# Where the low halves of the x forms are made, and which pairs take seven products: five edits to a decoder trunk in fp32

## The chip, the cores and the metric

One core of a Trainium2 chip. Its engines run each its own list of instructions and wait for each other through semaphores: PE (TensorE, matrix products), DVE (VectorE), ACT (ScalarE), POOL (GpSimd) and SP, which here only issues transfers. POOL and ACT issue transfers too. The metric is the device time of one execution in us; the lower the better.

## The reference

Two layers on 256 tokens of width 2048, all in fp32. Each is a token mixer (layer 0 HGRN2, layer 1 gated linear attention, GLA) beside a 4-head attention into 256 memory tokens, an output projection, and a SwiGLU feed-forward block (FFN) of width 5632:

```python
def reference(x, mem, ...):
    h = x
    for layer in range(2):
        hn = _rmsnorm(h, norm_mix[layer])
        y, xq = _hgrn2_mixer(hn, ...) if layer == 0 else _gla_mixer(hn, ...)
        xa = _memory_attention(xq, mem_n, w_mem_kv[layer])
        h = h + jnp.concatenate([y, xa], axis=-1) @ w_out[layer]

        hn = _rmsnorm(h, norm_ffn[layer])
        gate, up = jnp.split(hn @ w_gate_up[layer], 2, axis=-1)
        h = h + (jax.nn.silu(gate) * up) @ w_down[layer]
    return _rmsnorm(h, norm_final)
```

w_out is 2048 x 2048, w_gate_up 2048 x 11264, w_down 5632 x 2048; GLA's q and k are 768 columns each of its input projection.

## The kernel before

**Split operands.** PE multiplies a rounded form of fp32. So each operand is held as a high half (a rounded copy, made on ACT) and a low half (what the copy lost: a subtraction on DVE), and each product is three matmuls: xh by hi, xh by lo, xl by hi. A matmul takes 128 rows of K, one of the two tiles of 128 tokens and 512 columns of a weight (384 in GLA's q and k). This holds for weights (tiles "parts", line 300 and what calls it) and for activations.

**Pairs of K tiles and seven products.** 2048 rows of K are 16 tiles, taken as eight pairs 0 to 7. A pair's two K tiles, the two token tiles and two groups of columns (c0 and c1) are a product of 2 x 2 by 2 x 2 blocks. As eight products it costs 24 matmuls. As seven (Winograd's form of Strassen's scheme) it costs 21, for which sums and differences of the blocks are needed on both sides: of x once, of the weights for each pair and column group. A plan is a string that names the kind of each pair:

- "-": eight products; the four weight blocks are split in two operations each on ACT and on DVE (parts ..a, ..b).
- "S": seven products. `seven` splits one block (..a, 512 elements), two blocks (..b, 1024), then makes sums of blocks within the raw tile (512 and 1024 elements), and splits these (..c and ..d, 1024 each). Of pair 0's weights one sum comes from a load that accumulates into a tile T (POOL's queue).
- "H" and "O", in the FFN only: eight products that go into the same seven accumulators as S's, with a sum of weight blocks (H: ..a, ..b, a difference of 512, ..c of 512) or none (O).

The sums of a plan's S pairs share their accumulators, and after the last pair DVE adds these up into the four results (`early` in the output projection, `sums` in the FFN).

**The x forms of the FFN.** For each of the eight pairs `Forms` holds the four blocks of x and their sums and differences (eight forms for S, six for O, nine for B) with a high and a low half each, as PAIRS = "SSSSSOSB" says. `put` (line 394) gets the transposed blocks from PSUM, scales them on ACT into a staging tile g (tag "stg", two buffers), adds on DVE, makes the high half with one cast on ACT (hf_ph) and the low half with one subtraction on DVE (hf_pl). In names hf_3l is pair 3's low half. `h_forms` makes two pairs from 512 columns of h, as they come out of the output projection.

**The output projection.** In each layer: columns 0 to 511 by plain products (`one(0, ...)`, accumulators wo_0), then columns 512 to 1535 as pairs by the plan OUT (wo0p and wo1p), then columns 1536 to 2047 (`one(3, ...)`, wo_3), whose two sums are added into h by DVE as h<-wo_3. The forms of pairs 0 and 1 are made during the paired part, those of 2 to 5 during wo_3, and those of 6 and 7 need h's last columns, so they come during the first pairs of FFN block 0. For an S pair of OUT, the sums of the mixer's output y are made by `more_of`.

**The FFN.** `ffn` runs 11 blocks of 512 columns of gate and of up (`up_block`, accumulators f_p), each with the eight pairs in order by KINDS (one string for each of blocks 0 to 3, the last for 4 to 10). Weight pairs are numbered through the program: in layer 0 block 0 is parts84 (pair 0) to parts91 (pair 7), block 1 begins with parts92; in layer 1 block 0 is parts288 to 295. Between the blocks come parts of the down projection (fd). At the end of layer 0's FFN the last columns of the down projection go into h, and `h_quad` squares, transposes (tp_hm) and splits them for GLA's first projection (gx).

**What sets the order.** From pair 3 of block 0 on (`Engine.kept`, up to the end of the FFN's blocks), instructions keep the order of the code. Elsewhere a scheduler orders each engine's list at build time by its own estimate of times; in an engine's list an instruction that waits holds all that follow it. Small pieces of work are put in a queue (`later`), and `step`, called once or more for a pair, takes one off, or nothing where None was queued. Raw weight tiles have three buffers, the split "parts" six. Loads are issued by SP, except those that accumulate, which are POOL's.

## Time and profile before

| | |
|---|---|
| time before, median of 3 runs | 2253.98 us (2252.5 to 2254.8) |
| the profiled execution: own time, span | 2254.6 us, 2252.8 us |
| PE busy, matmuls | 2238.6 us (99%), 10668 |
| DVE busy, instructions | 2031.5 us (90%), 2551 |
| ACT busy, instructions | 1452.8 us (64%), 2010 |
| POOL busy, instructions | 280.4 us (12%), 275 |
| moved by DMA | 477.28 MB, mean 212 GB/s |
| mean granted clock of PE | 0.999 |

The span is that from the first to the last instruction. The busy time of an engine is the sum over its instructions, without those that issue transfers. Nearly every operation is recorded under line 151, a helper, so rows are told apart by the names of their tiles. A stage's state is read from the busy time in a stretch of the span, and from the waits in brackets: [0.49 <-ACT parts85b] means that an instruction's engine was idle 0.49 us before it and that ACT's result parts85b ended that.

### The profile page before, as it was taken

How to read it: one execution, taken by the hardware profiler on the slowest of the kernel's cores; microseconds unless marked ns; L12 is line 12 of the kernel's file. 1: busy time of each engine (PE TensorE's matmuls, PEld its weight loads, DVE VectorE, ACT ScalarE, POOL GpSimd, SP SyncE). 2: the span in 40 equal slices, each digit the busy share in tenths (PEclk: the TensorE clock that was granted, in tenths of full speed). 3: DMA queues.
4: the chain of work that ended last, by engine and by line, in shares of the span. 5: the costliest groups of instructions: out<-in, count | busy, mean ns of one | idle time of the engine just before them, and what ended most of it. 6: DMA issues, size and time to landing. Idle time of an engine off the chain costs nothing.

```text
span 2252.8 us, 30400 instructions
## 1 busy us (share of the span) xinstructions
PE 2238.6 (99%) x10668; PEld 1894.6 (84%) x10668; DVE 2031.5 (90%) x2551; ACT 1452.8 (64%) x2010; POOL 280.4 (12%) x275
## 2 busy tenths in 40 slices
PE   9999999999999999999999999999999999999998
PEld 7888888888888888888889999988888888888887
DVE  6879899898998999999996887889999999999997
ACT  7656656565666666666665665566566676666664
POOL 1000100000111112112210000000011221212110
PEclk9999999999999999999999999999999999999999
DMA  8656655656687778878865445566677878887874
GB/s 296 215 168 213 199 182 177 200 193 190 198 236 232 229 234 231 230 230 238 244 221 168 141 156 182 164 209 197 208 221 224 233 230 238 242 238 236 231 233 167
DMA packets 255628, 477.28 MB, mean 212 GB/s; under 512 B 18255, under 2 KB 47731, under 8 KB 255219
## 3 DMA queue, kind: packets, MB, share of 16 engines
q1 hardware_dynamic: 228547, 420.21, 55.5%
q0 software_dynamic: 25632, 50.87, 13.0%
q10 hardware_dynamic: 1296, 4.26, 0.5%
q8 instruction: 84, 1.38, 0.2%
q14 instruction: 69, 0.57, 0.1%
HBM read 472.12 MB, written 3.15 MB: 211 GB/s over the span
## 4 chain that ended last, share of the span: by engine, by line
PE 90%; DVE 6%; issue 2%; DMA 1%; ACT 1%; SPq 0%; POOL 0%; DVEq 0%; POOLq 0%; ACTq 0%
PE f_p L151 34%; PE fd L151 18%; PE wo L151 4%; PE m1p L151 2%; PE hv2p L151 2%; PE hv1p L151 2%; PE hf0p L151 2%; PE hv0p L151 2%; PE wo1p L151 2%; PE hf2p L151 2%; PE hf1p L151 2%; PE wo0p L151 2%; PE m0p L151 2%; PE gk0p L151 1%; PE gk1p L151 1%
## 5 line engine op out<-in xcount | busy, mean ns | idle before, releaser
L151 DVE TENSOR_TENSOR raw<-raw 128x1024 f32<-128x1024 f32 (+3 forms) x330 | 311.2, 943 | 16.7 <-DMA raw<-in_w_down_dram 5.6
L151 ACT CAST parts<-raw 128x1024 fp32r<-128x1024 f32 (+1 forms) x216 | 211.7, 1016 | 56.8 <-DMA raw<-in_w_down_dram 14.7
L151 DVE TENSOR_TENSOR parts<-raw,parts 128x1024 fp32r<-128x1024 f32 (+1 forms) x176 | 200.2, 1171 | 22.7 <-ACT parts L151 22.0
L444 POOL DMA_DIRECT2D raw<-in_w_gate_up_dram x92 | 80.4, 873 | 541.2 <-DMA raw<-in_w_gate_up_dram 274.7
L300 POOL TENSOR_TENSOR parts<-raw,parts 128x1024 fp32r<-128x1024 f32 x40 | 95.6, 2406 | 113.5 <-ACT parts L151 81.2
L151 ACT COPY h<-fd 128x512 f32<-128x512 f32 x80 | 45.7, 588 | 46.5 <-PE fd L151 44.0
L428 POOL DMA_DIRECT2D T<-in_w_gate_up_dram x36 | 21.1, 587 | 430.2 <-DVE hf_4g L151 82.7
L151 ACT ACTIVATE s<-s,rf_r 128x512 f32<-128x512 f32 x44 | 31.8, 723 | 42.0 <-DVE s L151 42.0
L151 DVE SCALAR_TENSOR_TENSOR s<-e,rf_r,s 128x512 f32<-128x512 f32 x44 | 45.7, 1076 | 2.9 <-ACT s L151 0.5
L151 DVE TENSOR_TENSOR e<-f_p,e 128x512 f32<-128x512 f32 x66 | 45.2, 684 | 2.6 <-DVE s L151 0.5
L429 POOL DMA_DIRECT2D T<-in_w_gate_up_dram x36 | 31.0, 861 | 120.4 <-DMA T<-in_w_gate_up_dram 111.1
L151 ACT COPY fd<-h 128x512 f32<-128x512 f32 x82 | 45.2, 582 | 0.0
L444 POOL DMA_DIRECT2D raw<-in_hgrn_w_in_dram x17 | 14.7, 867 | 209.9 <-DMA raw<-in_hgrn_w_in_dram 124.6
L151 PE MATMUL fd<-parts,s_0h 128*128 128x512 f32 x128 | 39.8, 392 | 0.0
L151 PE MATMUL fd<-parts,s_4h 128*128 128x512 f32 x128 | 39.8, 392 | 0.0
L151 PE MATMUL fd<-parts,s_8h 128*128 128x512 f32 x128 | 39.8, 392 | 0.0
L151 PE MATMUL fd<-parts,s_2h 128*128 128x512 f32 x128 | 39.8, 392 | 0.0
L151 PE MATMUL fd<-parts,s_6h 128*128 128x512 f32 x128 | 39.8, 392 | 0.0
L151 PE MATMUL fd<-parts,s_1h 128*128 128x512 f32 x128 | 39.4, 389 | 0.0
L151 PE MATMUL fd<-parts,s_3h 128*128 128x512 f32 x128 | 39.4, 389 | 0.0
L151 PE MATMUL fd<-parts,s_5h 128*128 128x512 f32 x128 | 39.4, 389 | 0.0
L151 PE MATMUL fd<-parts,s_7h 128*128 128x512 f32 x128 | 39.4, 389 | 0.0
(6020 smaller groups left out, 7434.0 us busy)
## 6 DMA issues: line engine op xcount, KB each, us to landing
raw<-in_w_gate_up_dram SPq DMA_DIRECT2D x224, 512.0 KB, 4.4
raw<-in_w_down_dram SPq DMA_DIRECT2D x80, 1024.0 KB, 5.5
raw<-in_w_gate_up_dram SPq DMA_DIRECT2D x220, 256.0 KB, 4.2
raw<-in_hgrn_w_in_dram SPq DMA_DIRECT2D x79, 512.0 KB, 4.6
raw<-in_gla_w_in_dram SPq DMA_DIRECT2D x96, 384.0 KB, 3.3
raw<-in_w_gate_up_dram POOLq DMA_DIRECT2D x92, 256.0 KB, 4.9
T<-in_w_gate_up_dram POOLq DMA_DIRECT2D x72, 256.0 KB, 5.0
raw<-in_w_out_dram SPq DMA_DIRECT2D x16, 1024.0 KB, 5.1
```

Source lines behind the costliest of these rows:

```text
L151: ins = func(*args, **kwargs)
L300: low = (nc.gpsimd if free_port else ve).tensor_tensor(out=both[:, 1, k:j, 0:m], in0=src[:, k:j, :], in1=both[:, 0, k:j, 0:m].bitcast(F32) ...
L428: nc.gpsimd.dma_start(out=both[:, 0, :], in_=rows[0])
L429: nc.gpsimd.dma_start(out=both[:, 0, :], in_=rows[1], accum_op=ALU.add)
L444: nc.gpsimd.dma_start(out=raw[:, 1, 0:n], in_=rows[1], accum_op=ALU.add)
```

## The change

Five edits:

1. In `Forms.put`, for kinds S and O (pairs 0 to 6), ACT writes -g into the low half beside the high half's sum, rounded as the high half is, and a DMA on POOL's queue, from SBUF to SBUF, then adds g to it. DVE's subtraction stays for pair 7 (kind B) alone. A transfer is 512 KB, for pair 5 (O) 384 KB. Since g has to live until its transfer has read it, the staging tiles of pairs 4, 5 and 6 are now tiles of other stages that are idle then ("v", "gate", "tq").
2. At the end of layer 0's FFN a None is queued ahead of the transposes of the third group of 512 columns, so these come a step later on PE.
3. GLA's q and k projections: one more pair is S, in both of them.
4. FFN block 0: pairs 2 and 4 go from H to S, in both layers.
5. The output projection: pair 7 of the plan goes from "-" to S, in both layers; the fourth S pair's forms of y are made by the `more_of` that is there, in the tile "Q".

```diff
--- before.py
+++ after.py
@@ -374,7 +374,7 @@
 
 
         def __init__(self, p, name):
-            self.kind = PAIRS[p]
+            self.p, self.kind = p, PAIRS[p]
             self.names = FACTORS[self.kind]
             n = len(self.names)
             th, tl = HOMES[p]
@@ -393,7 +393,9 @@
 
         def put(self, ps, gains):
 
-            g = work.tile([P, 8, P], F32, tag="stg", name=f"{self.name}g", bufs=2)
+            home = ("stg",) * 4 + ("v", "gate", "tq", "stg")
+            g = (opp if home[self.p] == "tq" else work).tile([P, 8, P], F32, tag=home[self.p], name=f"{self.name}g",
+                                                             **({"bufs": 2} if home[self.p] == "stg" else {}))
             for k in range(2):
                 ac.activation(out=g[:, 2 * k:2 * k + 2, :], in_=ps[:, 2 * k * P:(2 * k + 2) * P].rearrange(
                     "p (a t) -> p a t", t=P), func=AF.Copy, scale=gains[k])
@@ -401,7 +403,11 @@
 
             def parts(i, j, n):
                 ac.copy(out=self.h[:, i:i + n, :], in_=g[:, j:j + n, :])
-                tt(out=self.l[:, i:i + n, :], in0=g[:, j:j + n, :], in1=self.h[:, i:i + n, :].bitcast(F32), op=ALU.subtract)
+                if self.kind == "B":
+                    tt(out=self.l[:, i:i + n, :], in0=g[:, j:j + n, :], in1=self.h[:, i:i + n, :].bitcast(F32), op=ALU.subtract)
+                    return
+                ac.activation(out=self.l[:, i:i + n, :], in_=g[:, j:j + n, :], func=AF.Copy, scale=-1.0)
+                nc.gpsimd.dma_start(out=self.l[:, i:i + n, :].bitcast(F32), in_=g[:, j:j + n, :], accum_op=ALU.add)
 
             if self.kind == "O":
                 tt(out=g[:, 4:6, :], in0=g[:, 1:3, :], in1=g[:, 0:4:3, :], op=ALU.subtract)
@@ -672,7 +678,7 @@
     MANY = 12
 
 
-    def h_quad(hq, q, gain, ss, name, queue=later, sevens=SEVEN):
+    def h_quad(hq, q, gain, ss, name, queue=later, sevens=SEVEN, wait=False):
 
         for t in range(NT):
             square_sum(h[:, t, q * 512:(q + 1) * 512], ss[:, t, q:q + 1], f"{name}{q}{t}")
@@ -686,7 +692,7 @@
             hq[q] = Pairs(*both)
             hq.setdefault("pairs", {}).update({2 * q: both[0], 2 * q + 1: both[1]})
 
-        queue(turn)
+        queue(*([None] if wait else []), turn)
 
     def h_forms(forms, n, gain, ss, name):
 
@@ -1111,7 +1117,7 @@
                 nc.gpsimd.memset(dst[-1][:, :, :, DK:T], 0.0)
             return [lambda t, d=d: d[:, t, :, 0:DK] for d in dst]
 
-        project_two(hq["pairs"], ("------S-", "------S-")[pr], w, kw + pr * 2 * DK, pr * 2 * DK, 2 * DK, f"gk{pr}", give,
+        project_two(hq["pairs"], "-----SS-", w, kw + pr * 2 * DK, pr * 2 * DK, 2 * DK, f"gk{pr}", give,
                     lambda ps: ps.rearrange("p (a c) -> p a c", c=DK), fed=False)
         for d in dst:
             for t in range(NT):
@@ -1194,7 +1200,7 @@
     PARTS = ((0,), (1, 2), (3, 4), (5, 6), (7, 8), (9, 10))
 
 
-    KINDS = ("SHHSHOSO", "HHHSSOSO", "SHHSSOSO", "SSHSSOHS", "SSSSSOSS")
+    KINDS = ("SHSSSOSO", "HHHSSOSO", "SHHSSOSO", "SSHSSOHS", "SSSSSOSS")
 
 
 
@@ -1309,7 +1315,7 @@
 
     ENDS = (('0-1S2S3-',), ('0-1S2S3-',))
 
-    OUT = "4-5-2-0S6S7-3S1-"
+    OUT = "4-5-2-0S6S7S3S1-"
 
 
     flush()
@@ -1350,7 +1356,7 @@
         ss = new_ss(f"ss_n{l}")
         if l == 0:
             hq = {}
-            ffn(0, hq2, r2, lambda n: h_quad(hq, n, g_mix[1], ss, "hm1_", sevens=2))
+            ffn(0, hq2, r2, lambda n: h_quad(hq, n, g_mix[1], ss, "hm1_", sevens=2, wait=n == 2))
             scale = lambda ss=ss: h_scale(ss, "rm1", True)
         else:
             gf = []
```

(In OUT a digit is the pair, the sign behind it the kind: "7-" becomes "7S". The tile names y_7g and y_7m come from that part of y.)

The instructions move with it. First DVE in layer 0, at the end of the output projection and the beginning of block 0. Before:

```order
L151 SCALAR_TENSOR_TENSOR parts84c<-raw_4383,parts84c 128x512
L151 TENSOR_TENSOR parts84d<-raw_4383,parts84d 128x1024
L151 TENSOR_TENSOR hf_4l<-hf_4g,hf_4h 128x1024
L151 TENSOR_TENSOR hf_5l<-hf_5g,hf_5h 128x768
L151 TENSOR_TENSOR parts85a<-raw_4444,parts85a 128x1024
L151 TENSOR_TENSOR parts85b<-raw_4444,parts85b 128x1024
L151 TENSOR_TENSOR h<-wo_3_0_0_4179,h 128x512
L151 TENSOR_TENSOR h<-wo_3_0_1_4180,h 128x512
L151 TENSOR_TENSOR raw_4444<-raw_4444 128x512
L151 TENSOR_TENSOR parts86a<-raw_4499,parts86a 128x1024
L151 TENSOR_TENSOR parts85c<-raw_4444,parts85c 128x512
```

Now:

```order
L151 TENSOR_TENSOR raw_4405<-raw_4405 128x1024
L151 TENSOR_TENSOR h<-wo_3_0_0_4197,h 128x512
L151 TENSOR_TENSOR h<-wo_3_0_1_4198,h 128x512
L151 SCALAR_TENSOR_TENSOR parts84c<-raw_4405,parts84c 128x512
L151 TENSOR_TENSOR parts84d<-raw_4405,parts84d 128x1024
L151 TENSOR_TENSOR parts85a<-raw_4467,parts85a 128x1024
L151 TENSOR_REDUCE rf_red<-ss_f_3589 128x2
L151 TENSOR_TENSOR parts85b<-raw_4467,parts85b 128x1024
L151 TENSOR_SCALAR rf_v<-rf_red 128x2
L151 TENSOR_TENSOR parts86b<-raw_4522,parts86b 128x1024
```

parts84c's second half, parts84d, 85a and 85b stood ahead of the two adds h<-wo_3 and now stand behind them; the low halves hf_4l and hf_5l are gone. Three rows further on DVE's list now reads, with pair 86 as S:

```order
L151 SCALAR_TENSOR_TENSOR hf_6g<-hf_6g 128x128
L151 TENSOR_TENSOR hf_6g<-hf_6g 128x128
L151 TENSOR_TENSOR parts85c<-raw_4467,parts85c 128x512
L151 TENSOR_TENSOR parts86a<-raw_4522,parts86a 128x512
L151 TENSOR_TENSOR raw_4522<-raw_4522 128x512
L151 TENSOR_TENSOR raw_4522<-raw_4522 128x1024
L151 TENSOR_TENSOR hf_7g<-hf_7g 128x256
L151 SCALAR_TENSOR_TENSOR parts86c<-raw_4522,parts86c 128x1024
L151 SCALAR_TENSOR_TENSOR hf_7g<-hf_7g 128x128
L151 TENSOR_TENSOR parts86d<-raw_4522,parts86d 128x1024
L151 TENSOR_TENSOR hf_7g<-hf_7g 128x128
L151 TENSOR_TENSOR parts87a<-raw_4562,parts87a 128x512
```

No low half of hf_6 stands there any more; pair 86 takes six operations where as H it took four, and 88 likewise; parts88c comes 13 rows behind the last one shown.

Then ACT at the forms of pair 6 (hf_6hl holds both its halves). Before:

```order
L151 CAST parts85c<-raw_4444 128x512
L151 ACTIVATE junk_hf_31_4371,ss_f_3589<-h 128x512
L151 CAST parts86b<-raw_4499 128x1024
L151 ACTIVATE hf_6g<-tp_hf_6_4431,pv 128x256 x2
L151 CAST parts86c<-raw_4499 128x512
L151 CAST hf_6hl<-hf_6g 128x1024
L151 CAST parts87a<-raw_4536 128x512
L151 ACTIVATE hf_7g<-tp_hf_7_4483,pv 128x256 x2
L151 CAST parts87b<-raw_4536 128x1024
```

Now:

```order
L151 CAST parts85b<-raw_4467 128x1024
L151 CAST parts86b<-raw_4522 128x1024
L151 ACTIVATE hf_6g<-tp_hf_6_4453,pv 128x256 x2
L151 CAST parts85c<-raw_4467 128x512
L151 CAST hf_6hl<-hf_6g 128x1024
L151 ACTIVATE hf_6hl<-hf_6g 128x1024
L151 CAST parts86a<-raw_4522 128x512
L151 ACTIVATE hf_7g<-tp_hf_7_4506,pv 128x256 x2
L151 ACTIVATE parts86c<-raw_4522 128x1024
```

ACT makes both halves of hf_6, and the cast of 86a stands behind them; before, 86a's stood at the head, ahead of 85c's and 86b's.

## The prediction

> **What bounds the kernel now.** The totals come first, then the chain of waits, then the busy time by stage.
>
> ```profile
> PE 2238.6 (99%) x10668; PEld 1894.6 (84%) x10668; DVE 2031.5 (90%) x2551; ACT 1452.8 (64%) x2010; POOL 280.4 (12%) x275
> PE 90%; DVE 6%; issue 2%; DMA 1%; ACT 1%; SPq 0%; POOL 0%; DVEq 0%; POOLq 0%; ACTq 0%
> ```
>
> TensorE (PE) is busy 99% of the span and carries 90% of the chain that ends last, so a matmul taken away is worth its own time, as long as its operands come as early as they did. VectorE (DVE) at 90% makes nearly all of the operands. An average of 90% hides stages that are full:
>
> ```profile
> 462.00:493.00 31.00, 31.00 (x140) 25.71 (x139) 29.42 (x37) 20.07 (x24) 0.86 (x1) 1.00 0.64 211
> 493.00:517.00 24.00, 24.00 (x115) 19.78 (x114) 23.36 (x32) 17.14 (x29) 2.30 (x3) 1.00 0.56 182
> 517.00:560.00 43.00, 43.00 (x194) 35.37 (x193) 37.30 (x48) 26.55 (x36) 1.61 (x2) 1.00 0.64 202
> 1232.00:1276.00 44.00, 44.00 (x254) 42.87 (x253) 33.93 (x59) 28.10 (x48) 1.09 (x3) 1.00 0.43 140
> 1370.00:1395.00 25.00, 25.00 (x148) 24.97 (x148) 17.70 (x25) 13.70 (x19) 0.00 (x0) 1.00 0.59 189
> ```
>
> The columns are the stretch in us, its length, then PE, PEld, DVE, ACT and POOL busy, the granted clock, the DMA share and GB/s. In layer 0 the first three rows are the paired output projection, its last quarter with the make-up of the FFN's x forms, and FFN block 0. The last two are GLA's two k/q projections. PE never idles in any of them, and the clock is full. DVE has 1.58 us of idle time in the first, 0.64 in the second and 5.70 in the third, but 10.07 and 7.30 in GLA's. So the change takes PE work from places of two kinds, and in the first DVE has next to nothing to give.
>
> **What goes from PE.** The pace is read from the chain's runs of matmuls and the places where the chain leaves PE:
>
> ```profile
> 505.99 10.93 PE wo L151 x48
> 516.92 4.76 PE f_p L151 x21
> 522.12 5.51 PE f_p L151 x24
> 544.43 6.79 DMA raw<-in_w_gate_up_dram
> 584.26 18.45 PE f_p L151 x80
> 1241.93 4.16 PE gk0p L151 x24
> ```
>
> 10.93/48 = 0.228 us for one of 512 columns (4.76/21 = 0.227), 4.16/24 = 0.173 for one of 384. A pair as S takes 21 matmuls, as H or "-" 24. Block 0 gets two more S pairs in each layer: 12 matmuls. The output projection gets one more: 6. Together 18 × 0.227 = 4.09 us. GLA's plan gets one more S pair in each of two projections: 6 × 0.173 = 1.04. In all 5.13 us. The first row is the end of the output projection, the next two are pairs 0 and 1 of block 0; the chain leaves PE after pair 1 and comes back in block 1, by way of transfers that no wait of PE shows.
>
> **The wait at the end of layer 0's FFN.** Two transposes now stand one step later on PE:
>
> ```profile
> PE tp_hm L151 <- DVE h L151: 1.0, 2, 0.8
> 1195.64 0.39 PE L151 MATMUL fd<-parts,s_9l 128*128 128x512 f32 x1
> 1196.82 0.30 PE L151 MATMUL tp_hm<-ident,h 128*128 128x128 f32 x1 [0.80 <-DVE h L151]
> 1197.33 0.33 PE L151 MATMUL tp_hm<-turned_id,h 128*128 128x128 f32 x1 [0.21 <-DVE h L151]
> ```
>
> From 1195.64 to 1196.82 are 1.18 us where the pace is 0.23, and from 1196.82 to 1197.33 0.51 where the next transposes stand 0.11 apart: 0.95 + 0.40, so about 1.3 us of PE idle time. What PE now does in between is 12 of its own matmuls (2.7 us), so the adds into h are done by then. What comes later is the use of these two x pairs, at the head of GLA's first projection; 24 matmuls (5.4 us) still lie ahead of it. I take −1.3, with 0 and −1.35 as ends.
>
> **What the S pairs cost DVE.** These rows of DVE's time order give the prices and the place:
>
> ```profile
> 503.33 1.22 DVE L151 TENSOR_TENSOR hf_2l<-hf_2g,hf_2h 128x1024 fp32r<-128x1024 f32 x1
> 512.75 0.95 DVE L151 TENSOR_TENSOR hf_5l<-hf_5g,hf_5h 128x768 fp32r<-128x768 f32 x1
> 513.62 1.22 DVE L151 TENSOR_TENSOR parts85a<-raw,parts85a 128x1024 fp32r<-128x1024 f32 x1
> 515.33 1.22 DVE L151 TENSOR_TENSOR parts85b<-raw,parts85b 128x1024 fp32r<-128x1024 f32 x1 [0.49 <-ACT parts85b L151]
> 516.47 1.28 DVE L151 TENSOR_TENSOR h<-wo,h 128x512 f32<-128x512 f32 x2
> 517.67 0.68 DVE L151 TENSOR_TENSOR raw<-raw 128x512 f32<-128x512 f32 x1
> 518.26 1.22 DVE L151 TENSOR_TENSOR parts86a<-raw,parts86a 128x1024 fp32r<-128x1024 f32 x1
> 519.40 0.68 DVE L151 TENSOR_TENSOR parts85c<-raw,parts85c 128x512 fp32r<-128x512 f32 x1
> 525.76 1.23 DVE L151 TENSOR_TENSOR hf_6hl<-hf_6g,hf_6hl 128x1024 fp32r<-128x1024 f32 x1 [1.17 <-ACT hf_6hl L151]
> ```
>
> By start to start, 1024 elements cost 1.14 us (518.26 to 519.40), 512 cost 0.60 (517.67 to 518.26), 768 cost 0.87; 256 and 128 I take as 0.34 and 0.20 on the same line. S needs 0.60 + 1.14 + 0.60 + 3 × 1.14 = 5.76 us of DVE for 21 × 0.227 = 4.77 of PE; H needs 2 × 1.14 + 2 × 0.60 = 3.48, "-" 2 × 1.14 = 2.28, both for 5.45. So an S pair runs DVE into arrears by 1.0 us, where an H pair let it gain 2.0 and "-" 3.2.
>
> In a GLA projection the added pair costs DVE (5.76 − 2.28) × 384/512 = 2.6 us, against 10.07 and 7.30 of idle time; nothing is late, and the 1.04 stands.
>
> The x forms hand DVE time back: per layer the low halves of pairs 0 to 6, 6 × 1.14 + 0.87 = 7.7 us. They go to ACT (an operation as long as the cast, 1.0 us) and to a POOL DMA that accumulates within SBUF.
>
> ```profile
> T<-in_w_gate_up_dram POOLq DMA_DIRECT2D x72, 256.0 KB, 5.0
> q0 software_dynamic: 25632, 50.87, 13.0%
> 524.68 1.05 ACT L151 CAST hf_6hl<-hf_6g 128x1024 fp32r<-128x1024 f32 x1 [1.17 <-DVE hf_6g L151]
> ```
>
> No such transfer is in the trace. A load of 256 KB by POOL's queue lands after 5.0 us; half the bytes of these, so I bound it by 5 and 10 us. Pair p's forms are first used when PE gets there: with S, H, S, S, S, O ahead, at 516 + 10.2 for pair 2 and 516 + 30 for pair 6, while hf_2's low half was made at 503 and hf_6's at 526. That leaves 20 us or so for each. I cost the latency at nothing. In the second row 50.87 MB take 13.0% of 2252.8 us, 5.8 us of all 16 engines for a MB, so a layer's 3.4 MB of forms take about 20 us spread over 60, at a DMA share of 0.56 to 0.64.
>
> **Where the lead is lost.** The given-back time falls mostly before the end of the output projection, and DVE can't keep it as a lead. Before, parts84c, 84d, 85a and 85b stood ahead of the two adds that take wo_3 out of PSUM (h<-wo at 516.47). By the new order the second half of 84c, 84d, 85a and 85b stand behind them, and these adds can't start until PE ends wo_3, about 515.6 if it ends 0.7 earlier. From there to the end of 87c, in the order shown, DVE has 1.20 (h) + 0.60 + 1.14 (84d) + 2.28 (85a, b) + 0.39 (rf) + 1.14 (86b) + 0.74 (hf_6g) + 1.20 (85's sum and c) + 0.60 (86a) + 0.60 + 1.14 (86's sums) + 2.28 (86c, d) + 0.74 (hf_7g) + 1.74 (87a, b) + 1.14 (hf_7l) + 0.20 + 1.74 (87's sums) + 1.14 (87c) = 20.0 us: done at 535.6. PE needs 87c after 21 + 24 + 21 + 9 matmuls (17.1) and the transposes of pairs 6 and 7 (0.9, 8 each at 0.11): 516.1 + 18.0 = 534.1. So it waits 1.5. To the end of 88c come 0.20 + 1.14 + 0.60 + 1.14 + 0.60 + 1.14 + 1.14 = 5.96 more, done at 541.6; PE, without a wait, is there 21 matmuls later, at 538.9. The stall is **at least 2.7 us in a layer**, above the 9 × 0.227 = 2.04 which the layer saves. Then pair 5 (O) lets DVE catch up.
>
> That takes ACT's results as always ready. In layer 0 ACT now makes hf_6's high and low half ahead of 86a's cast, after DVE's last hf_6g: 0.96 + 0.96 + 0.53 us and two hand-overs of about 0.1, while DVE has only 85c (0.60): 2.1 us of waiting, 4.8 in all. In layer 1 86's counterpart (290a) is cast first, and ACT's two halves delay only 290c, by some 0.6 behind DVE's two sums: 3.3.
>
> In the paired output projection pair 7 adds 3.48 and its y forms some 2.0 (two operations of 512 and four of 128), and hf_0 and hf_1 take 2.28 away: 3.2 us more for a DVE with 1.58 idle in 31. The excess of 1.6 lands on PE unless DVE's lead at 462 covers it. In layer 0 the low parts of pair 6 stand behind an add that waits for PE, so I take half, 0.7, there; none in layer 1, where they don't; the ends are 0 and 1.6 each.
>
> **The sum**, against the profiled execution, whose own time is 2254.6, 0.6 above the median of 2253.98: −5.13 − 1.3 + 4.8 + 3.3 + 0.7 = **+2.4 us**, so 2257.0 there and **2256.4** as a median.
>
> **The rivals.**
> 1. *Only the bare stall.* ACT's results are ready, and the output projection loses nothing: −6.4 + 2 × 2.7 = −1.0, so 2253. For it: the third window leaves ACT 16 us idle in 43. Against: before, DVE waited for ACT in this very place (0.49 and 1.17 in the rows above).
> 2. *DVE keeps its lead.* The stall isn't there, because the adds of wo_3 come early enough or the shorter operations overlap better than start to start says: −6.4 us, 2247.6. For it: outside GLA DVE loses 15 us of lows in the two layers and takes on 20 (four pairs by 2.3, two by 5.5), 2.4 a layer, less than the 7.9 us which it has idle in the first three windows. Against: the walk above, in which no step is a wait other than for PE's own end.
> 3. *The transfers collide.* Four of the accumulating transfers go out between 500 and 515, 2.0 MB together, by the price above 11 us of all 16 engines in 15, while the weights of pairs 84 to 86 come in; with a share of 0.56 for these the engines are some 4 us behind at its end. The b columns of 86 are accumulated by the same POOL queue, behind hf_5's transfer. A form or a weight landing later than about 525 stops PE: with 86 late by 3 us in each layer, +2.4 + 6 = 2262. It decides from a DMA share near 1 in this stretch. For it: that arithmetic. Against: 86's second load, issued about 512, has some 13 us before DVE needs it, and 5.0 is the price, 9 with the backlog. The Trainium skill ("Trainium Kernel Development and Optimization", Key Constraints) says that DMAs from the SP, ACT and POOL queues run on the same 16 engines and interleave; by that, a second queue brings no capacity, which speaks for this rival, and no run so far shows it for accumulation within SBUF.
> 4. *The change doesn't do what it says*: no. The order has the seven lows of each layer gone from DVE and seven DMAs on POOL, and the fewer matmuls.
>
> **How the numbers follow.** The forecast gets 0.44, the bare stall 0.19, the lead kept 0.17, the collision 0.20. What can be told from no change here is about 0.2%, 4.5 us, so 2249.5 to 2258.5. Of the forecast's 0.44 I put 0.30 within, 0.13 slower and 0.01 faster, since ACT's waits and the output projection are the softest terms; of the bare stall 0.15 within and 0.04 faster; of the lead kept 0.15 faster and 0.02 within; of the collision 0.18 slower and 0.02 within. Faster 0.20, same 0.49, slower 0.31. The range 2250.0 to 2262.5 leaves out most of the kept lead and the far end of the collision.
>
> **What would show it.** PE's busy time down by about 5 us, and the tp_hm wait gone. In block 0 of both layers the chain should pass from PE to DVE or ACT between pairs 2 and 4, with PE waiting for parts86a, 87c and 88c; DVE should stand idle just before h<-wo, and be full from there to 88d. ACT should have no wait longer than now at the forms' low halves. If PE has no wait for DVE or ACT in block 0, my walk is wrong and the time is near 2248; if PE waits there for a transfer or an hf low half, the third rival holds.

## The result

The changed kernel takes **2267.97 us** (median of 5, 2267.09 to 2269.32) where the kernel before took 2253.98: a ratio of 1.0060, 95% interval 1.0049 to 1.0070, so **14 us slower**. I had forecast no change at 2256.4, with a range of 2250.0 to 2262.5. The forecast was wrong, and the range missed the time by 5.5 us.

The totals of the profile after, and its chain of waits by engine:

```profile
PE 2240.1 (99%) x10644; PEld 1890.1 (83%) x10644; DVE 2041.3 (90%) x2575; ACT 1475.2 (65%) x2038; POOL 300.7 (13%) x295
PE 86%; DVE 5%; DMA 3%; ACT 3%; issue 2%; SPq 0%; POOL 0%; POOLq 0%; DVEq 0%; ACTq 0%
```

PE has fewer matmuls than before, but its share of the chain fell from 90% to 86%; DMA has 3% instead of 1%, ACT 3% instead of 1%. Where the time went is best seen by laying the two traces' starts of stages beside each other (the first matmul of a stage; the span is 2252.8 before and 2265.3 now):

| stretch | before, us | after, us | change |
|---|---|---|---|
| start to the first output projection (wo0p) | 445.58 | 447.09 | +1.51 |
| layer 0: paired output projection | 47.44 | 47.76 | +0.32 |
| layer 0: last quarter (wo_3) | 23.74 | 23.58 | -0.16 |
| **layer 0: FFN block 0** | 42.61 | 48.18 | **+5.57** |
| layer 0: the other blocks, to GLA's gx | 646.98 | 645.77 | -1.21 |
| GLA, to wo1p | 287.48 | 286.41 | -1.07 |
| layer 1: paired output projection, last quarter | 66.20 | 66.54 | +0.34 |
| **layer 1: FFN block 0** | 42.65 | 48.37 | **+5.72** |
| layer 1: the other blocks, to the last matmul | 642.62 | 642.66 | +0.04 |
| from there to the end | 7.52 | 8.95 | +1.43 |

The two block 0 are 11.3 us. The first and the last row, 2.9 us, I do not put down to the change: in the profiles of the experiments the first stretch is 0 to 2.8 us longer than before and the last 0 to 1.4, also in kernels that alter nothing there. The two profiled executions took 2254.6 and 2267.09 us, 12.5 apart; the 14.0 is between the medians.

PE's waits in the changed kernel, the longest first (us in total, times, the longest):

```profile
PE f_p L151 <- DVE parts291c L151: 1.9, 1, 1.9
PE f_p L151 <- ACT parts291c L151: 1.6, 1, 1.6
PE f_p L151 <- ACT parts87c L151: 1.4, 1, 1.4
...
PE f_p L151 <- DVE parts87c L151: 0.9, 1, 0.9
PE f_p L151 <- DVE parts290c L151: 0.8, 1, 0.8
...
PE f_p L151 <- DVE parts88c L151: 0.8, 1, 0.8
...
PE f_p L151 <- ACT parts86a L151: 0.6, 1, 0.6
```

They are the weights of pairs 2 to 4 of block 0 in both layers (86 to 88, 290 to 291), as the prediction's walk had it, and the wait at tp_hm is gone. But they are longer. The busy times of the stages that answer to those of before (us, length, PE, PEld, DVE, ACT, POOL, clock, DMA share, GB/s):

```profile
493.00:517.00 24.00, 24.00 (x115) 20.03 (x115) 18.23 (x30) 20.50 (x33) 3.45 (x4) 1.00 0.78 219
517.00:560.00 43.00, 38.53 (x164) 29.14 (x163) 39.91 (x50) 29.57 (x39) 7.07 (x8) 1.00 0.89 243
1588.00:1593.00 5.00, 3.97 (x10) 3.12 (x11) 4.96 (x8) 1.58 (x4) 0.00 (x0) 0.66 0.70 235
```

In the last quarter of the output projection DVE is now busy 18.23 us of 24, down from 23.36, and ACT 20.50, up from 17.14. The time that edit 1 freed on DVE is spent waiting. DVE's rows there, those with a wait, and its arrival at the adds of wo_3:

```profile
510.08 0.43 DVE L151 TENSOR_TENSOR hf_5g<-hf_5g 128x256 f32<-128x256 f32 x1 [3.71 <-ACT hf_5g L151]
511.02 1.22 DVE L151 TENSOR_TENSOR parts<-raw,parts 128x1024 fp32r<-128x1024 f32 x1 [0.51 <-ACT parts L151]
513.43 1.23 DVE L151 TENSOR_TENSOR parts<-raw,parts 128x1024 fp32r<-128x1024 f32 x1 [1.19 <-ACT parts L151]
...
518.65 1.28 DVE L151 TENSOR_TENSOR h<-wo,h 128x512 f32<-128x512 f32 x2
...
523.03 1.23 DVE L151 TENSOR_TENSOR parts85b<-raw,parts85b 128x1024 fp32r<-128x1024 f32 x1 [0.16 <-ACT parts85b L151]
525.14 1.23 DVE L151 TENSOR_TENSOR parts86b<-raw,parts86b 128x1024 fp32r<-128x1024 f32 x1 [0.81 <-ACT parts86b L151]
...
530.47 0.70 DVE L151 TENSOR_TENSOR parts86a<-raw,parts86a 128x512 fp32r<-128x512 f32 x1 [1.78 <-ACT parts86a L151]
```

DVE does not wait for PE at h<-wo: it gets there at 518.65, when PE has just begun block 0 (its first matmul is at 518.43). It had waited for ACT earlier, 3.71 + 0.51 + 1.19 us. What ACT was doing:

```profile
503.50 1.07 ACT L151 CAST hf_2h<-hf_2g 128x1024 fp32r<-128x1024 f32 x1
504.45 1.08 ACT L151 ACTIVATE hf_2l<-hf_2g 128x1024 fp32r<-128x1024 f32 x1
505.41 1.06 ACT L151 CAST hf_3h<-hf_3g 128x1024 fp32r<-128x1024 f32 x1
506.34 1.08 ACT L151 ACTIVATE hf_3l<-hf_3g 128x1024 fp32r<-128x1024 f32 x1
507.30 1.06 ACT L151 CAST hf_4h<-hf_4g 128x1024 fp32r<-128x1024 f32 x1
508.24 1.08 ACT L151 ACTIVATE hf_4l<-hf_4g 128x1024 fp32r<-128x1024 f32 x1
509.20 0.84 ACT L151 ACTIVATE hf_5g<-tp_hf,pv 128x256 f32<-128x256 f32 x2
509.92 1.07 ACT L151 CAST parts<-raw 128x1024 fp32r<-128x1024 f32 x1
```

Six copies of x forms in a row, three of them (hf_2l, hf_3l, hf_4l) edit 1's, stand ahead of the cast of wo_3's weights, and DVE's low half of these weights (511.02) and all of 84 and 85 follow behind.

The transfers landed late too. From the issues between 500 and 530, first after, then before (KB each, us from issue to landing):

```profile
raw<-in_w_gate_up_dram SPq DMA_DIRECT2D x6, 512.0 KB, 7.7
...
hf_2l<-hf_2g POOLq DMA_DIRECT2D x1, 512.0 KB, 6.2
hf_3l<-hf_3g POOLq DMA_DIRECT2D x1, 512.0 KB, 9.2
hf_4l<-hf_4g POOLq DMA_DIRECT2D x1, 512.0 KB, 10.3
hf_5l<-hf_5g POOLq DMA_DIRECT2D x1, 384.0 KB, 9.5
```

```profile
raw<-in_w_gate_up_dram SPq DMA_DIRECT2D x7, 512.0 KB, 4.1
```

The forms' own transfers stayed within my bounds (5 to 10 us) or nearly, and none of them was late for PE. The weights beside them took 7.7 us where they took 4.1.

So two theories stood at the start of the experiments: **A**, edit 1 does the harm (its copies on ACT, its transfers), and **B**, block 0's two S pairs are more than DVE can do. Comparisons below are with runs of the kernel before on the same chip; as a common measure I give the recorded ratio to these with its 95% interval (it is near the quotient of the two medians, not equal to it), and for the state of DVE the time from block 0's first matmul to the end of DVE's parts85b (289b in layer 1). Before, that is -0.2 us in both layers: done just ahead of the block.

### The profile page after: what moved, and what is told of

The parts are those of the page before. It is cut to its first block, busy times and chain, and to the rows that moved or that the text cites. A ratio compares the mean times of both kernels' runs of the same rounds, so it can differ in the third digit from the quotient of the medians.

```text
span 2265.3 us, 30508 instructions
## 1 busy us (share of the span) xinstructions
PE 2240.1 (99%) x10644; PEld 1890.1 (83%) x10644; DVE 2041.3 (90%) x2575; ACT 1475.2 (65%) x2038; POOL 300.7 (13%) x295
## 3 DMA queue, kind: packets, MB, share of 16 engines
q8 instruction: 83, 1.36, 0.2%
## 4 chain that ended last, share of the span: by engine, by line
PE 86%; DVE 5%; DMA 3%; ACT 3%; issue 2%; SPq 0%; POOL 0%; POOLq 0%; DVEq 0%; ACTq 0%
PE f_p L151 33%; PE fd L151 19%; PE m1p L151 2%; PE hv2p L151 2%; PE hv1p L151 2%; PE hf0p L151 2%; PE hf2p L151 2%; PE hf1p L151 2%; PE fd_0p L151 2%; PE wo L151 2%; PE hv0p L151 2%; PE gg11p L151 1%; PE gg01p L151 1%; PE gg10p L151 1%; PE gk1p L151 1%
## 5 line engine op out<-in xcount | busy, mean ns | idle before, releaser
L151 DVE TENSOR_TENSOR raw<-raw 128x1024 f32<-128x1024 f32 (+2 forms) x344 | 324.0, 942 | 19.5 <-DMA raw<-in_w_down_dram 7.0
L450 POOL DMA_DIRECT2D raw<-in_w_gate_up_dram x96 | 87.2, 923 | 546.2 <-DMA raw<-in_w_gate_up_dram 250.0
```

The costliest lines, as they stand in the source:

```text
L151: ins = func(*args, **kwargs)
L450: nc.gpsimd.dma_start(out=raw[:, 1, 0:n], in_=rows[1], accum_op=ALU.add)
```

## The experiments

**One edit undone at a time.**

u1_forms, without edit 1:

```diff
-                ac.activation(out=self.l[:, i:i + n, :], in_=g[:, j:j + n, :], func=AF.Copy, scale=-1.0)
-                nc.gpsimd.dma_start(out=self.l[:, i:i + n, :].bitcast(F32), in_=g[:, j:j + n, :], accum_op=ALU.add)
+                tt(out=self.l[:, i:i + n, :], in0=g[:, j:j + n, :], in1=self.h[:, i:i + n, :].bitcast(F32), op=ALU.subtract)
```

> The changed kernel with edit 1 undone: the low halves of pairs 0 to 6 are subtractions on DVE again, no transfers within SBUF, staging in two buffers; edits 2 to 5 stay. Theory A (edit 1 itself does the harm: its casts stand ahead of the weights' casts on ACT, its transfers fill the DMA engines and stand ahead of the weights' accumulating loads in POOL's queue): the wait of 3.7 us of DVE for ACT in the last quarter of the output projection is gone, the DMA share in the 42 us from there on falls from about 0.95 to 0.6, block 0 costs no more than 3 us in a layer, time 2254 to 2260. Theory B (the two S pairs in block 0 are too much for DVE by themselves): DVE gets 7.7 us more work in a layer, so block 0 stalls at least as long as now, time 2267 to 2275.

Measured: 2260.84 (before 2255.72), ratio 1.0024 (1.0014 to 1.0033), 0.8 us above theory A's range. 85b ends 4.8 and 5.9 us into block 0, which is 3.0 and 3.8 us longer than before.

u4_block0, without edit 4:

```diff
-    KINDS = ("SHSSSOSO", "HHHSSOSO", "SHHSSOSO", "SSHSSOHS", "SSSSSOSS")
+    KINDS = ("SHHSHOSO", "HHHSSOSO", "SHHSSOSO", "SSHSSOHS", "SSSSSOSS")
```

> The changed kernel with edit 4 undone: block 0 is SHHSHOSO again, edits 1, 2, 3 and 5 stay. Theory B: block 0's stalls (6.1 and 6.6 us) go, while 12 matmuls (2.7 us) come back: 2268 - 12.7 + 2.7 = 2258. Theory A: the transfers still fill the DMA engines and the weights of pairs 1 to 3 still come late, so a wait of 2 to 4 us stays in each layer: 2262 to 2266.

Measured: 2263.00, ratio 1.0035 (1.0021 to 1.0048), within A's range. 85b ends 5.7 and 5.4 us into block 0.

u5_out, without edit 5:

```diff
-    OUT = "4-5-2-0S6S7S3S1-"
+    OUT = "4-5-2-0S6S7-3S1-"
```

> The changed kernel with edit 5 undone: the output projection has three S pairs again, edits 1 to 4 stay. Both theories: the paired part costs 0.3 and 0.45 us less than it does now, and block 0 is unchanged: 2267 to 2268. If the fourth S pair is what makes DVE late into the last quarter and so into block 0, 2262 to 2265.

Measured: 2259.54, ratio 1.0017 (1.0008 to 1.0026), below both ranges. 85b ends 0.2 and 2.1 us into block 0.

Theory B falls with the first: more work for DVE made the kernel faster. But A alone doesn't stand either: each of the three, taken out, gives back 40 to 70% of the loss (0.0036, 0.0025 and 0.0043 of 0.0060), together more than there is. Least expected was edit 5: I had put it at nothing, and without it the lead of DVE into block 0 is back in layer 0.

**Edits 2 and 3 alone** (a23_wait_gk).

```diff
-        project_two(hq["pairs"], ("------S-", "------S-")[pr], w, kw + pr * 2 * DK, pr * 2 * DK, 2 * DK, f"gk{pr}", give,
+        project_two(hq["pairs"], "-----SS-", w, kw + pr * 2 * DK, pr * 2 * DK, 2 * DK, f"gk{pr}", give,
-        queue(turn)
+        queue(*([None] if wait else []), turn)
```

> The kernel before with edits 2 and 3 alone (transposes one step later, one more S pair in GLA's q and k projections). Both theories: -1.4 at the end of layer 0's FFN and -0.95 in GLA as in the changed kernel's trace, 2251.6. It also tells whether the 1.5 us at the start and the 1.4 us at the end, by which the changed kernel's trace is longer outside the edited places, come and go from one program to the next.

Measured: 2253.81 (before 2255.72), ratio 0.9995 (0.9986 to 1.0004); by the medians 1.9 us are gained where 2.4 were expected. In its trace the end of layer 0's FFN is 1.38 us shorter and the two projections 0.40 and 0.52, as in the changed kernel. The gain isn't clear of the noise.

**Each of the other edits alone**, on the kernel before, the diffs those above the other way round.

o1_forms_only, edit 1:

> The kernel before with edit 1 alone (low halves by ACT and an accumulating transfer); no pair changes its kind. Theory A (the casts on ACT and the transfers are harm by themselves): DVE waits some 3 to 4 us for ACT in the last quarter of the output projection, the DMA share from there on is above 0.8, block 0 loses 1 to 4 us in a layer: 2256 to 2262. Theory B (DVE's work decides): DVE has 7.7 us less to do in a layer, no stall, 2253.5 to 2254.5.

Measured: 2256.17 (before 2255.14), ratio 1.0002 (0.9993 to 1.0012); block 0 is as long as before (42.62 and 42.59), 85b ends 0.2 us into it. DVE waits for ACT here too:

```profile
506.85 0.43 DVE L151 TENSOR_TENSOR hf_4g<-hf_4g 128x256 f32<-128x256 f32 x1 [2.80 <-ACT hf_4g L151]
...
512.41 0.69 DVE L151 SCALAR_TENSOR_TENSOR parts84c<-T,parts84c 128x512 fp32r<-128x512 f32 x1 [1.40 <-ACT parts84c L151]
```

but the wait costs nothing: 84c to 85b still stand ahead of the adds of wo_3 in this list, 85b is 0.4 us later than before, and block 0 has its H pairs. Edit 1 alone does no harm that can be told from the noise.

o4_block0_only, edit 4:

> The kernel before with edit 4 alone (pairs 2 and 4 of block 0 as S), the low halves on DVE as before. Theory A: nothing else stands in the way, so 12 matmuls are saved and DVE's arrears cost at most as much: 2251 to 2255. Theory B: before, 87c comes just in time; as S pair 2 costs DVE 2.3 us more and PE 0.7 less, pair 4 the same again, so 87c is 3 us late and 88c another 2 to 3; less the 1.36 saved that is 3 to 5 us a layer: 2260 to 2264.

Measured: 2258.65, ratio 1.0013 (1.0003 to 1.0022). 85b ends at -0.2 us as before, and block 0 is 43.23 and 43.24 us long: 1.36 us of matmuls saved, 2.0 lost, nearly all of it in waits for 87c and 88c (PE's matmuls there start 0.7 and 1.0 us late); the time lies between the two ranges. Even with DVE's lead whole the two S pairs don't pay. DVE ends 87c 18.84 us into the block in both kernels and 88c at 24.92, where it was 24.61: PE comes there earlier and waits.

o5_out_only, edit 5:

> The kernel before with edit 5 alone (fourth S pair in the output projection). The paired part has DVE at 95% and gets 5.5 us more of it, so it ends level or up to 1.6 us later in each layer; what DVE then has not done in time passes on to block 0. If block 0 takes it up in its H pairs: 2253 to 2255; if the lead into block 0 is gone, 2 to 3 us a layer: 2258 to 2261.

Measured: 2258.02, ratio 1.0012 (1.0003 to 1.0022). The paired output projection takes 1.0 and 1.55 us longer, six matmuls fewer notwithstanding, and 85b ends 4.3 and 4.6 us into block 0. Its H pairs absorb that (42.62 and 42.89 us), so the time is in the second range, but the loss is in the paired part, not in block 0. The paired part in this kernel, layers 0 and 1:

```profile
462.00:493.00 31.00, 30.54 (x135) 24.21 (x134) 31.00 (x39) 20.71 (x25) 0.86 (x1) 1.00 0.47 141
1505.00:1536.00 31.00, 29.96 (x132) 23.48 (x131) 30.91 (x37) 19.97 (x24) 1.72 (x2) 1.00 0.63 189
```

DVE is busy 31.00 us of 31 and 30.91 of 31. What doesn't fit is pushed on into the last quarter, and so into block 0. Here is what I had missed: the paired part had 1.6 us left, I let at most that much land on PE, and did not carry the rest over as lateness.

The four ratios of single edits less 1, each with an interval of about 0.001 either way, sum to 0.0022 (5 us); all together make 0.0060 (13.5 us). More than half the loss lies in their combination, above all that of edits 1 and 5: by the singles these two make 0.0009 with 2 and 3, while u4_block0, which has just these four, measured 0.0035. Edit 5 makes DVE 4.5 us late, edit 1 takes 7.7 us a layer off DVE, and yet with edit 5 there 85b is no earlier (5.8 and 5.4 us with edit 1, 4.8 and 5.9 without).

**What of edit 1 does that: ACT's copies or the transfers?** Two kernels each take one of them away.

y3_no_transfer:

```diff
-                nc.gpsimd.dma_start(out=self.l[:, i:i + n, :].bitcast(F32), in_=g[:, j:j + n, :], accum_op=ALU.add)
```

> The changed kernel without the accumulating transfers of the low halves: ACT's second copy stays, so the low halves keep -g and the products with them are wrong. It takes away the transfers' load on the DMA engines and in POOL's queue, nothing else; the scheduler orders DVE's list as in the changed kernel. Theory T (the transfers hold up the weights): the DMA share after the output projection is back at 0.6, waits for late weights go, 2255 to 2260. Theory S (ACT's second copies stand ahead of the weights' casts, so DVE starts block 0 5.8 us late): 85b still ends 5 to 6 us after block 0's start, 2264 to 2267.

Measured: 2263.49 (before 2255.79), ratio 1.0036 (1.0023 to 1.0049). The lists of DVE and ACT are the changed kernel's, row for row, so this difference is the transfers'; the time lies between the two ranges, 0.5 us under S's. 85b ends 5.8 and 5.3 us into block 0, as in the changed kernel (5.8 and 5.4); 87c 22.7 and 20.7 us into it, against 23.7 and 23.6. The stretch from 506 and that from 1554, with the transfers (the changed kernel) and then without:

```profile
506.00:518.00 12.00, 12.00 (x55) 9.94 (x54) 6.59 (x9) 10.03 (x14) 3.28 (x4) 1.00 0.95 213
1554.00:1566.00 12.00, 12.00 (x55) 9.91 (x54) 7.76 (x10) 9.21 (x13) 2.59 (x3) 1.00 1.04 235
```

```profile
506.00:518.00 12.00, 12.00 (x55) 9.93 (x54) 7.08 (x9) 9.21 (x14) 0.84 (x2) 1.00 0.53 168
1554.00:1566.00 12.00, 12.00 (x56) 9.90 (x55) 6.59 (x8) 10.37 (x15) 0.00 (x0) 1.00 0.45 144
```

The DMA share falls by a half. The transfers cost some 5 us of the 14 (0.0060 - 0.0036 = 0.0024; by the two intervals 2 to 9 us). The two block 0 of the traces are 0.95 and 3.0 us shorter without them, by late weights within block 0, in layer 1 above all. The two profiled executions as a whole are only 1.8 us apart, since other stages are longer in this one, GLA by 2.0 and the output projection of layer 1 by 1.55.

y2_no_act_copy:

```diff
-                ac.activation(out=self.l[:, i:i + n, :], in_=g[:, j:j + n, :], func=AF.Copy, scale=-1.0)
-                nc.gpsimd.dma_start(out=self.l[:, i:i + n, :].bitcast(F32), in_=g[:, j:j + n, :], accum_op=ALU.add)
+                nc.gpsimd.dma_start(out=self.l[:, i:i + n, :].bitcast(F32), in_=g[:, j:j + n, :])
```

> The changed kernel without ACT's second copy: the low half is written by a plain transfer of g, so it is g itself and the products with it are wrong. The transfers and their place in POOL's queue stay (without the accumulation), ACT has seven operations less in a layer. Theory T: little changes, 2262 to 2267. Theory S: no wait of 3.7 us of DVE for ACT in the last quarter of the output projection, 85b ends within 1 us of block 0's start, only the two S pairs' own arrears stay (1 to 2 us a layer), 2253 to 2258.

Measured: 2260.12, ratio 1.0018 (1.0009 to 1.0028), between the two ranges. 85b ends 0.0 and 0.9 us into block 0: the lead is back, with edit 5 in place. Layer 0, where block 0 begins at 518.36:

```profile
517.18 1.22 DVE L151 TENSOR_TENSOR parts85b<-raw,parts85b 128x1024 fp32r<-128x1024 f32 x1
518.31 1.28 DVE L151 TENSOR_TENSOR h<-wo,h 128x512 f32<-128x512 f32 x2
```

Block 0 is 43.23 and 44.06 us long, nearly o4_block0_only's. So without ACT's second copies, edit 1 does pay for edit 5's work; with them it does not. The transfers are plain ones here, but y3_no_transfer, which has none, shows that 85b's lateness is not theirs. By which way the copies do it stays open: with them gone the scheduler also lists 84c to 85b ahead of the adds of wo_3 again, as the two rows show, so the effect is that of the waits for ACT and of the order together. The order can do it without the copies: in u1_forms and o5_out_only, whose low halves are DVE's, the adds also stand ahead of 84d, 85a and 85b.

The two shares, 9.5 us without the copies (0.0060 - 0.0018 = 0.0042) and 5 without the transfers, can't be added up: they overlap. In y2_no_act_copy, too, the weights' 512 KB landed late (7.3 us between 500 and 530, 7.7 in the changed kernel), and yet block 0 of layer 0 is as long as in o4_block0_only, which has no such transfers, and that of layer 1 0.8 us longer. So the copies make DVE late at block 0's start, and late weights cost time within it where DVE has no lead.

**Two attempts to mend it, and one to go further.**

y5_lows_later:

```diff
+                def low():
                     ac.activation(out=self.l[:, i:i + n, :], in_=g[:, j:j + n, :], func=AF.Copy, scale=-1.0)
                     nc.gpsimd.dma_start(out=self.l[:, i:i + n, :].bitcast(F32), in_=g[:, j:j + n, :], accum_op=ALU.add)
+                if 2 <= self.p <= 5:
+                    lows.append(low)
...
         later(lambda: turn(2 * n), lambda: turn(2 * n + 1))
+        if n == 2:
+            later(*[lambda: lows.pop(0)()] * 4)
```

> The changed kernel, complete, with the low halves of pairs 2 to 5 (ACT's second copy and the transfer) queued as pieces of their own behind all four pairs' high halves, so that ACT's list has the last weights of the output projection ahead of most of them, and the transfers go out later. Theory S: DVE waits less for ACT, 85b ends at most 3 us after block 0's start, 2256 to 2262. Theory T: the transfers now lie closer to the use of weights and forms, 2266 to 2272.

Measured: 2277.61, ratio 1.0097 (1.0082 to 1.0112), and neither theory's reason. PE's longest wait in each layer:

```profile
PE f_p L151 <- ACT parts291a L151: 6.4, 1, 6.4
PE f_p L151 <- ACT parts87a L151: 6.4, 1, 6.4
```

The four new pieces of the queue push the forms of pairs 6 and 7 back by one step. From pair 3 on the code's order is kept, and pair 7's forms now stand in ACT's list ahead of the casts of 87: these wait for transposes that PE makes only after pair 2. As a test of the copies' place it says nothing beyond 85b, which ends 4.7 and 4.5 us into the block in place of 5.8 and 5.4.

x_pool_lows:

```diff
-                ac.activation(out=self.l[:, i:i + n, :], in_=g[:, j:j + n, :], func=AF.Copy, scale=-1.0)
-                nc.gpsimd.dma_start(out=self.l[:, i:i + n, :].bitcast(F32), in_=g[:, j:j + n, :], accum_op=ALU.add)
+                nc.gpsimd.tensor_tensor(out=self.l[:, i:i + n, :], in0=g[:, j:j + n, :],
+                                        in1=self.h[:, i:i + n, :].bitcast(F32), op=ALU.subtract)
```

> The changed kernel, but the seven low halves of a layer are subtractions on POOL in place of a cast on ACT and a transfer: no transfers within SBUF, ACT and DVE both without these operations. Theory A: both harms are gone, DVE's lead into block 0 is back, stalls of at most 1.5 us a layer: 2250 to 2254. Theory B: DVE's list in block 0 is what it is in the changed kernel, so the stalls stay near 4 to 6 us a layer: 2262 to 2267. If POOL's operations (2.4 us each for 1024 elements by the weights' ones) hold up the loads behind them in its queue, in between.

Measured: 2284.23, ratio 1.0124 (1.0109 to 1.0139), slower than every expectation. 85b ends 9.1 and 8.5 us into block 0; the last section shows what POOL's operations did to DVE's.

b1_gla_three goes on from edits 2 and 3:

```diff
-            ffn(0, hq2, r2, lambda n: h_quad(hq, n, g_mix[1], ss, "hm1_", sevens=2, wait=n == 2))
+            ffn(0, hq2, r2, lambda n: h_quad(hq, n, g_mix[1], ss, "hm1_", sevens=3, wait=n == 2))
-        project_two(hq["pairs"], "-----SS-", w, kw + pr * 2 * DK, pr * 2 * DK, 2 * DK, f"gk{pr}", give,
+        project_two(hq["pairs"], "----SSS-", w, kw + pr * 2 * DK, pr * 2 * DK, 2 * DK, f"gk{pr}", give,
```

> The kernel before with edits 2 and 3, and one step on: a third pair's forms are made at the end of layer 0's FFN, and GLA's q and k plans have three S pairs (----SSS-). All theories: GLA's projections are the place where DVE had 10 and 7 us idle, so 6 matmuls of 384 columns more go, 1.0 us, and the forms cost DVE some 3.5 us at the end of layer 0's FFN, where it was 60 to 70% busy: 2250 to 2253 where before is 2254 to 2255.5. If the forms make the first GLA projection wait, the gain at the end of the FFN (1.4) is gone and it is 2253 to 2255.

Measured: 2256.89 (before 2255.62), ratio 1.0003 (0.9994 to 1.0012), above both ranges. The first projection is 1.07 us shorter than before, as expected, but then comes a new wait:

```profile
PE slg L151 <- DVE Tg L151: 2.5, 1, 2.5
```

What PE gained, DVE did not have ready for GLA's scores, which come behind the projection. No version found is clearly faster than the kernel before; edits 2 and 3 alone are the best, at 0.9995.

## Why the prediction was wrong

The step that failed is the size of the stall in block 0, 4.8 and 3.3 us in the sum and 6.9 and 7.1 in the trace, and in it the transfers, whose effect on the weights beside them the sum had at nothing. Where PE would wait, for the weights of pairs 2 to 4, was right. Term by term:

- **The matmuls removed** (-5.13): right. GLA's two projections gained 0.43 and 0.52 in the trace, 0.95 where 1.04 was forecast. But the sign given for it failed: PE's busy time did not fall by 5 us, it rose by 1.5 (2238.6 to 2240.1), in part because a matmul that stands alone behind a wait counts more (0.49 us at 1586.59 in the last section) than one in a row (0.227).
- **The wait at tp_hm** (-1.3): -1.43 in the trace, so right for that pair of executions. But in the traces of o1_forms_only and o5_out_only, which lack edit 2, there was no such wait, and in o4_block0_only there was (1.6 us). The gain is one that only some executions have to give.
- **The output projection** (+0.7 in layer 0, none in layer 1, less the 0.68 saved): the mechanism was right, its size and its reach were not. The trace has +0.32 and +0.45, that is 1.0 and 1.1 lost in each. The sum had no term for the lateness that this work carries on to block 0, 4.3 to 4.6 us with edit 5 alone; the walk through block 0 came to a lateness of that size by the order of the list.
- **"Where the lead is lost"**: the place and nearly the size came out, the sign did not. By the walk 85b would have ended about 5 us into block 0 in both layers; it was 5.8 and 5.4. But DVE was to stand idle at h<-wo until PE was done, and it came there at 518.65 with no wait for PE, because ACT had kept it waiting for 5.4 us before, which the walk had not. The runs do not rule out the order as the cause. In o5_out_only DVE does wait for PE at these adds, until 0.48 us before block 0 begins; the changed kernel comes there 0.70 us after that point, 0.26 in layer 1. So with the adds where they stand, the waits for ACT made 85b later by no more than that, and its 5.8 and 5.4 us would have been some 5.1 by the order alone. y2_no_act_copy, at 0.0 and 0.9, took away the waits and the order together.
- **The stall in block 0** (4.8 and 3.3): it was 5.57 + 1.36 = 6.9 and 5.72 + 1.36 = 7.1. Of the 2.1 and 3.8 us missing, y3_no_transfer gives 0.95 and 3.0 to the transfers, and 0.8 and 0.4 are those by which 85b is later than in the walk; 0.4 in each layer are left. Behind 85b, in layer 1, it allowed 0.6 us of waiting, and weights landing late brought more:

```profile
1572.42 1.23 DVE L151 TENSOR_TENSOR parts290b<-raw,parts290b 128x1024 fp32r<-128x1024 f32 x1 [1.64 <-ACT parts290b L151]
...
1578.91 1.23 DVE L151 SCALAR_TENSOR_TENSOR parts290c<-raw,parts290c 128x1024 fp32r<-128x1024 f32 x1 [0.49 <-ACT parts290c L151]
...
1584.76 1.95 DVE L151 TENSOR_TENSOR raw<-raw 128x512 f32<-128x512 f32 x2 [1.01 <-DMA raw<-in_w_gate_up_dram]
```

  (the cast of 290b itself waited 1.89 us for its load). In layer 0 the wait for 86a behind hf_6's two halves was 1.78, where I had 2.1: right. (The walk's "8 each" for the transposes of pairs 6 and 7 are 4 each in the trace; its 0.9 us is that of the eight.)
- **The transfers** ("I cost the latency at nothing"): right for the forms, wrong for the weights beside them. The third rival had the price (the engines 4 us behind) and gave 2262 for it at a chance of 0.20; it was no rival but came on top of the forecast, some 5 us. The Trainium skill's sentence that these queues share 16 engines and interleave ("Trainium Kernel Development and Optimization", Key Constraints) agrees with the weights' 7.7 us in place of 4.1.
- The sum, by the trace: +2.4 forecast, 2.1 and 3.8 more in the two block 0, 0.3 and 1.1 in the two paired projections, 2.9 at the start and the end (not put down to the change), -0.1 in the rest, is 12.5, the difference of the two executions. The range was built as if the forecast and the collision excluded each other; they came together.

## What to carry to other kernels

Before work is moved from a full engine to one that looks half idle, look at where in that engine's list it will stand: here 5.7 us of copies in a row, half of them new, on an ACT at 64% went ahead of the casts on which the full engine lived, and freed time became waiting time. When an engine has no slack in a stage, what is added there is not lost at its end but carried as lateness to the next stage that needs a lead, so follow the end of one fixed operation against the consumer's start through every stage. And test edits singly and with one left out: these were about +0.5, +2.9 and +2.7 us apart (and -1.1 for the rest), and +14 together.

## What the runs showed of the hardware

**A subtraction on POOL holds up DVE's operations on two inputs in SBUF.** In x_pool_lows, POOL's rows and then DVE's during them:

```profile
508.75 5.59 POOL L409 TENSOR_TENSOR hf_2l<-hf_2g,hf_2h 128x1024 fp32r<-128x1024 f32 x1 [30.88 <-ACT hf_2h L151]
514.30 3.38 POOL L409 TENSOR_TENSOR hf_3l<-hf_3g,hf_3h 128x1024 fp32r<-128x1024 f32 x1
```

```profile
512.49 2.93 DVE L151 TENSOR_TENSOR parts<-raw,parts 128x1024 fp32r<-128x1024 f32 x1 [0.41 <-ACT parts L151]
515.35 2.88 DVE L151 TENSOR_TENSOR parts84a<-raw,parts84a 128x512 fp32r<-128x512 f32 x1
518.15 2.61 DVE L151 TENSOR_TENSOR hf_5g<-hf_5g 128x256 f32<-128x256 f32 x1
520.68 0.68 DVE L151 TENSOR_TENSOR raw<-T,raw 128x512 f32<-128x512 f32 x1
```

512 elements took 2.88 us where the next operation of that size took 0.68, and 256 elements 2.61 where 0.42 is usual, while POOL's own took up to 5.6 us for the 2.4 of its operations elsewhere. The rows read as if one engine stands until the other's operation has ended: POOL's two end at 514.34 and 517.68, and the operations of DVE that had begun in them end 1.08 and 0.55 us later, as long as 1024 and 512 elements take by themselves. It isn't always DVE that stands: from 509.72 on two of its subtractions of 1024 took 2.36 us together, their usual pace, during POOL's 5.59. The kernel before shows the same on a smaller scale. POOL runs 40 such subtractions there. DVE's 96 operations of 512 elements that began during them with one input from PE's accumulators (e<-f_p,e and the like) took 0.70 us at most, as always. The 20 that read two inputs from SBUF (s<-e,rf_r,s) took 0.99 to 2.50 us where 0.74 is usual, and each ended 0.55 us after POOL's. The Trainium skill ("GPSIMD Engine Reference", Specifications) says that GpSimd shares its SBUF interfaces with VectorE, with contention for VectorE's instructions with two SBUF inputs; the runs agree, and give the size.

**PE fell to half pace after two waits.** In layer 1 of the changed kernel:

```profile
1586.59 0.49 PE L151 MATMUL f_p<-parts291c,hf_3h 128*128 128x512 f32 x1 [1.57 <-ACT parts291c L151]
1589.03 0.60 PE L151 MATMUL f_p<-parts291c,hf_3h 128*128 128x512 f32 x1 [1.95 <-DVE parts291c L151]
1589.44 0.63 PE L151 MATMUL f_p<-parts291c,hf_3l 128*128 128x512 f32 x1
...
1592.42 0.76 PE L151 MATMUL f_p<-parts291d,hf_3h 128*128 128x512 f32 x2
```

After waits of 1.57 and 1.95 us close together the matmuls start 0.43 us apart up to 1592.4, where 0.227 is the pace, with a granted clock of 0.66 in the row of 1588 to 1593 above. That is some 1.7 us more (nine steps, most 0.20 too long), which no term of the sum had. Little of it reached the time: DVE had 292c ready at 1595.26 only, and PE, slowed, came to the matmul that needs it at 1595.56. At its full pace it would have stood there, as it did 0.8 us for 88c in layer 0, so I estimate the cost from these two times at 0.3 us; block 0 is only 0.19 us longer in layer 1 than in layer 0. The Trainium skill ("TensorE: Matmul & The Clock Gate", Part 1) has the array's clock halved after an idle window of about 3.4 us, and 426.7 ns between matmuls of 512 then; the pace agrees, and here one matmul between two shorter waits did not prevent it.
